# Expert gates built from bfloat16 one-hots of 8 tokens, one PSUM copy moved to ScalarE, and two activation steps moved forward

## The chip, the core and the metric

The kernel runs on one core of a Trainium2 chip. The metric is device time in microseconds (us) of one execution, the median of several. The engines are TensorE (PE, with its weight loads listed apart as PEld), VectorE (DVE), ScalarE (ACT), GpSimd (POOL) and SyncE (SP), which only issues DMAs here.

## The reference, cut to what matters

Two transformer blocks on 512 tokens of width 1024. The first has attention over 512 tokens and 16 meta tokens, then a feed-forward layer. The second has two more attentions and ends in PEER, a layer of 16384 experts, of which every token picks 16 in each of 8 heads:

```python
def _peer(h, w_pq, sub_keys, peer_u, peer_v):
    qp = (h @ w_pq).astype(jnp.float32).reshape(b, s, PEER_HEADS, 2, PEER_HALF)
    sc = jnp.einsum("bshpd,hpnd->bshpn", qp, sub_keys.astype(jnp.float32))
    s1, i1 = lax.top_k(sc[..., 0, :], PEER_TOPK)
    s2, i2 = lax.top_k(sc[..., 1, :], PEER_TOPK)
    cand = (s1[..., :, None] + s2[..., None, :]).reshape(b, s, PEER_HEADS, PEER_TOPK * PEER_TOPK)
    top_s, top_c = lax.top_k(cand, PEER_TOPK)
    e1 = jnp.take_along_axis(i1, top_c // PEER_TOPK, axis=-1)
    e2 = jnp.take_along_axis(i2, top_c % PEER_TOPK, axis=-1)
    expert = e1 * N_KEYS + e2                      # N_KEYS = 128
    gate = jax.nn.softmax(top_s, axis=-1)
    ...
    a = jnp.einsum("bcd,bchkd->bchk", h_c, peer_u[expert])
    w = gate * jax.nn.gelu(a)
    return jnp.einsum("bchk,bchkd->bcd", w, peer_v[expert])
```

The kernel computes PEER in two ways. For the first 128 tokens it fetches the picked rows one at a time ("sparse"). For the other 384 it computes all 16384 experts as dense matrix products and multiplies the activations by a dense matrix of gates, which is zero where an expert was not picked.

## The kernel before, in words

Everything is written in one order by hand, per engine; each engine runs its own instructions in that order. The places that the change touches are four.

**Attention of the first block** (65 to 330 us of the span). `turn1` transposes a block of probabilities on PE: four tiles of 128 keys into the bank `ps` (line 848), and the 16 meta keys into a free corner `m` of the PSUM bank that held the scores (line 846). ACT copies the four tiles to `pt` (line 850) and DVE copies the corner to `pm` (line 849). Until `pm` is copied the scores of a later step, which need that bank (lines 821 and 832), cannot be written.

**Dense gates** (1251 to 1482 us). `dense_gates` runs three times, `t` = 1, 2, 3, for 128 tokens each; below these are the first, second and third run. At the start PE transposes the expert numbers and the gates of the 128 tokens (lines 1840 and 1841) and ACT copies them to `et` (line 1843). Then come 32 steps of four tokens. For each token the gates are an outer product: a matrix with a 1 at (e1, k) for pick k, times a matrix with the gate at (e2, k). `ones` makes both. DVE makes the first for four tokens in one instruction (line 1854) and the second for three of the four tokens (line 1859, compare and multiply in one); ACT makes the second of the fourth token from two instructions (lines 1862 and 1863). All are float32. PE multiplies them (line 1876, one matmul call per token, four calls into one bank, each with a step of four in the output), and ACT copies the bank to `stage` (line 1878), which goes to DRAM as `gd`. `ones` runs two steps (`LA`) ahead of the products.

Between the steps `_merge` puts PE work of another kind, the first activations: per step `QW` = 1.0 us of it by a planner's figure, which gives two or three groups of three matmuls `ua` (lines 368 to 370). These bring with them the casts of streamed weights, `wh` on ACT (line 225) and `wl` on DVE (line 227), and their `ga` on ACT (line 1777). The expert numbers of the next run (`experts`, lines 1946 to 1952) are spread over the first two runs, and the sparse rows (line 1971) begin in the third.

**The main loop** (1482 to 2340 us). 64 rounds; each adds one group of experts to the output with 36 matmuls `yres` (line 2052) in six steps of `v_phase`. The gated activations of the next round are split into two parts for this: ACT makes `wh_` (line 2030) at step n = 2 and DVE makes `wl_` (line 2031) at n = 4, counted from 0, each from the entry `at[n]`. In between `tick` puts in sparse rows.

**Set-up.** `peer` makes a row of the numbers 0 to 127 with POOL's `iota` (line 1633).

Of the kernel before, what the change touches and what calls it, by code (L numbers as in the profile page):

```python
# [278 lines left out]
class Program:  # L279
# [561 lines left out]
    def turn1(self, p, pt, pm, s2):  # L841

        nc = self.nc
        ps = self.bank((P, 4, P), name="tp")
        m = s2[0:NMETA, 0, HK:HK + P]
        nc.tensor.transpose(out=m, in_=p[:, NTOK:NKEY], identity=self.ident)
        for j in range(4):
            nc.tensor.transpose(out=ps[:, j, :], in_=p[:, j * P:j * P + P], identity=self.ident)
        nc.vector.tensor_copy(out=pm[0:NMETA], in_=m)
        nc.scalar.copy(out=pt, in_=ps)  # L850
# [768 lines left out]
    def peer(self):  # L1619
# [11 lines left out]
        self.first_products(self.norm2, pss, pc["pq"], self.rest)  # L1631
        self.iota = self.ph.tile([P, P], F32, name="iota")
        nc.gpsimd.iota(self.iota, pattern=[[1, P]], base=0, channel_multiplier=0, allow_small_or_imprecise_dtypes=True)
        self.iota16 = self.ph.tile([P, 16, 8], BF16, name="iota16")
# [40 lines left out]
        for i in range(64):  # L1675
# [6 lines left out]
            if i < 63:  # L1682
# [8 lines left out]
                nxt = None  # L1691
            at = dict(zip((2, 4), todo[1:]))
            if i == 63:
# [90 lines left out]
    def gates(self, val, idx, found, keys):  # L1784
# [11 lines left out]
        for t in range(4):  # L1796
            yield from self.best_sums(val, top, topc, t)
            if t == 0:
                yield from self.softmax(top[:, 0:1], gt[:, 0:1], 2.5)
                self.where(topc[:, 0:1], sel[:, 0:1])  # L1800
                yield 2.0
                ee = self.tmp([P, 2, 128], name="ee")
                yield from self.experts(sel[:, 0], ixf[:, 0], ee)
                self.sgate = self.ph.tile([P, P], F32, name="sgate")
# [8 lines left out]
        yield GY[0]  # L1813
        ee = self.tmp([P, 2, 128], name="ee")
        soft = self.softmax(top[:, 1:4], gt[:, 1:4], 3.0)
        yield next(soft)
        yield from self.experts(sel[:, 1], ixf[:, 1], ee)
        yield from soft
        yield 3.0
        for t in range(1, 4):  # L1820
            now, more = ee, None
            if t < 3:
                ee = self.tmp([P, 2, 128], name="ee")
                more = self.experts(sel[:, t + 1], ixf[:, t + 1], ee)
            for i, us in enumerate(self.dense_gates(t, now, gt[:, t], 0)):
                if t == 3:
                    self.tick(QR)
                yield us
                if more and i % 6 == 3:
                    us = next(more, None)  # L1830
                    if us:
                        yield us
        self.ahead(0)

    def dense_gates(self, t, ee, gt, first):
# [5 lines left out]
        nc.tensor.transpose(out=ps[:, 2, :], in_=gt, identity=self.ident)  # L1841
        et = self.tmp([P, 4, P], name="et")
        nc.scalar.copy(out=et[:, 0:3], in_=ps)
        nc.scalar.mul(out=et[:, 3], in_=ps[:, 2], mul=-1.0)
        todo = [(blk, q) for blk in range(first, 4) for q in range(8)]
        hot = {}

        def ones(n):

            blk, q = todo[n]  # L1850
            tk = blk * 32 + q * 4
            o1 = self.tmp([P, 4, P], name="o1")
            o2 = self.tmp([P, 4, P], name="o2")
            nc.vector.tensor_tensor(out=o1, in0=self.iota.unsqueeze(1).to_broadcast([P, 4, P]),
                                    in1=et[:, 0, tk:tk + 4].unsqueeze(2).to_broadcast([P, 4, P]), op=OP.is_equal)
            for i in range(4):
                e2, g, ng = (et[:, j, tk + i:tk + i + 1] for j in (1, 2, 3))
                if i < 3:
                    nc.vector.tensor_scalar(out=o2[:, i, :], in0=self.iota, scalar1=e2, scalar2=g,
                                            op0=OP.is_equal, op1=OP.mult)  # L1860
                else:
                    nc.scalar.activation(out=o2[:, i, :], in_=self.iota, func=AF.Abs, bias=e2, scale=-1.0)
                    nc.scalar.activation(out=o2[:, i, :], in_=o2[:, i, :], func=AF.Relu, bias=g, scale=ng)
            hot[n] = o1, o2

        for n in range(LA):
            ones(n)
        for n, (blk, q) in enumerate(todo):
            if q == 0:
                stage = [self.slot([P, 64, 32], name="stage") for _ in range(2)]  # L1870
            if n + LA < len(todo):
                ones(n + LA)
            o1, o2 = hot.pop(n)
            pg = self.bank((P, P, 4), name="pg")
            for i in range(4):
                nc.tensor.matmul(out=pg[:, :, i], lhsT=o1[:, i, :], rhs=o2[:, i, :], start=True, stop=True)  # L1876
            for e in range(2):
                nc.scalar.copy(out=stage[e][:, :, q * 4:q * 4 + 4], in_=pg[:, e * 64:e * 64 + 64, :])
            if q == 7:
                for e in range(2):  # L1880
                    nc.scalar.dma_start(out=self.gd[t * 4 + blk - NS // 32, e], in_=stage[e])
            yield QW
# [54 lines left out]

    def experts(self, sel, ixf, ee):

        nc = self.nc  # L1940
        for a in range(2):
            eq = self.slot([P, 16, 16, 8], BF16, name="eq")
# [155 lines left out]
```

## Time and profile before

| | |
|---|---|
| median of 3 runs | 2361.22 us (2353.3 to 2362.54) |
| the profiled execution | 2359.9 us, of which the span of its instructions is 2358.2 us |
| mean granted clock of TensorE | 0.983 of full speed |
| PE busy | 2251.2 us (95%) |
| PEld busy | 1984.5 us (84%) |
| DVE busy | 1682.3 us (71%) |
| ACT busy | 983.1 us (42%) |
| POOL busy | 833.6 us (35%) |

PE and PEld overlap, and busy shares are averages over stages that differ. What the stages of the change look like is read from their own stretches of the trace, in us from the start of the span.

### The profile page before, as it was taken

How to read it: one execution, taken by the hardware profiler on the slowest of the kernel's cores; microseconds unless marked ns; L12 is line 12 of the kernel's file. 1: busy time of each engine (PE TensorE's matmuls, PEld its weight loads, DVE VectorE, ACT ScalarE, POOL GpSimd, SP SyncE). 2: the span in 40 equal slices, each digit the busy share in tenths (PEclk: the TensorE clock that was granted, in tenths of full speed). 3: DMA queues.
4: the chain of work that ended last, by engine and by line, in shares of the span. 5: the costliest groups of instructions: out<-in, count | busy, mean ns of one | idle time of the engine just before them, and what ended most of it. 6: DMA issues, size and time to landing. Idle time of an engine off the chain costs nothing.

```text
span 2358.2 us, 33496 instructions
## 1 busy us (share of the span) xinstructions
PE 2251.2 (95%) x12511; PEld 1984.5 (84%) x12511; DVE 1682.3 (71%) x3461; ACT 983.1 (42%) x1896; POOL 833.6 (35%) x666
## 2 busy tenths in 40 slices
PE   6999989999999998999998999999999999999998
PEld 5787868888889777788997999988888888888997
DVE  7565665766635547567998889577877778887776
ACT  4454453322224456543436777433333333333332
POOL 3231411020021235222340002356665666665553
PEclk9999999999999999999998999999999999999999
DMA  4111113645523101222354557998889989999885
GB/s 174 37 55 36 72 36 99 243 180 208 190 94 121 56 21 55 90 90 90 124 187 158 215 226 261 323 334 305 314 326 332 332 318 320 319 328 330 315 295 190
DMA packets 137698, 459.82 MB, mean 195 GB/s; under 512 B 10256, under 2 KB 62800, under 8 KB 105536
## 3 DMA queue, kind: packets, MB, share of 16 engines
q1 hardware_dynamic: 91120, 276.86, 33.2%
q0 software_dynamic: 37920, 138.31, 16.4%
q10 hardware_dynamic: 8496, 42.52, 4.5%
q8 instruction: 98, 1.61, 0.3%
q14 instruction: 64, 0.52, 0.1%
HBM read 415.13 MB, written 42.47 MB: 194 GB/s over the span
## 4 chain that ended last, share of the span: by engine, by line
PE 31%; DVE 11%; issue 6%; POOL 3%; ACT 2%; DMA 1%; ACTq 0%; POOLq 0%; DVEq 0%
PE yres L2052 15%; PE ua L370 4%; PE ua L368 4%; PE ua L369 4%; PE pg L1876 3%; POOL rows L1964 2%; DVE wl L227 1%; DVE ys L1986 1%; DVE rest L1749 1%; POOL ga L2029 1%; ACT wh L225 1%; DVE idx L1753 1%; DVE idx L1747 1%; DVE rows L1971 1%; DVE val L1751 1%
## 5 line engine op out<-in xcount | busy, mean ns | idle before, releaser
L227 DVE TENSOR_TENSOR wl<-raw,wh 128x1024 fp32r<-128x1024 f32 x345 | 480.6, 1411 | 313.3 <-ACT wh L225 312.7
L225 ACT CAST wh<-raw 128x1024 fp32r<-128x1024 f32 (+1 forms) x398 | 405.0, 1039 | 326.7 <-PE yres L2052 155.4
L368 PE MATMUL ua<-ah,wh 128*128 128x384 f32 x1024 | 353.2, 345 | 0.0
L370 PE MATMUL ua<-ah,wl 128*128 128x384 f32 x1024 | 345.0, 337 | 2.6 <-POOL wl L227 1.9
L369 PE MATMUL ua<-al,wh 128*128 128x384 f32 x1024 | 344.6, 337 | 0.0
L1964 POOL DMA_INDIRECT rows<-in_eu_dram,sidx x128 | 184.6, 1442 | 417.7 <-DVE rows L1971 380.8
L1964 POOL DMA_INDIRECT rows<-in_ev_dram,sidx x128 | 193.1, 1509 | 167.5 <-DVE ys L1986 141.1
L370 PEld LDWEIGHTS ua<-ah,wl 128*128 128x128 f32 x1024 | 193.6, 189 | 3.3 <-POOL wl L227 2.2
L369 PEld LDWEIGHTS ua<-al,wh 128*128 128x128 f32 x1024 | 194.2, 190 | 1.4
L368 PEld LDWEIGHTS ua<-ah,wh 128*128 128x128 f32 x1024 | 194.1, 190 | 1.4
L1986 DVE SCALAR_TENSOR_TENSOR ys<-rows,sact,ys 128x1024 f32<-128x1024 f32 x127 | 177.0, 1394 | 1.8
L227 POOL TENSOR_TENSOR wl<-raw,wh 128x1024 fp32r<-128x1024 f32 (+2 forms) x53 | 118.6, 2246 | 151.8 <-ACT wh L225 145.0
L1777 ACT ACTIVATE ga<-ua 128x384 f32<-128x384 f32 x128 | 63.3, 494 | 256.2 <-PE ua L370 252.4
L2029 POOL TENSOR_TENSOR ga<-ga,gt 128x384 f32<-128x384 f32 x128 | 157.8, 1256 | 21.4 <-DMA ga<-sd 20.2
L1971 DVE SCALAR_TENSOR_TENSOR rows<-rows,hn 128x1024 f32<-128x1024 f32 x128 | 159.8, 1272 | 0.0
L368 PE MATMUL pj<-wh,ah 128*128 128x512 f32 (+3 forms) x344 | 128.3, 373 | 9.7 <-ACT ah L521 9.3
L368 PE MATMUL gu<-ah,wh 128*128 128x512 f32 x352 | 137.4, 390 | 0.0
L370 PE MATMUL gu<-ah,wl 128*128 128x512 f32 x352 | 137.0, 389 | 0.0
L369 PE MATMUL gu<-al,wh 128*128 128x512 f32 x352 | 136.9, 389 | 0.0
L1194 POOL TENSOR_TENSOR xr<-xr,dr 128x512 f32<-128x512 f32 x12 | 20.0, 1670 | 294.9 <-DVE dr L1192 294.9
L370 PE MATMUL pj<-wh,al 128*128 128x512 f32 (+3 forms) x344 | 121.3, 353 | 0.1
L369 PE MATMUL pj<-wl,ah 128*128 128x512 f32 (+3 forms) x344 | 120.8, 351 | 0.0
(907 smaller groups left out, 5468.3 us busy)
## 6 DMA issues: line engine op xcount, KB each, us to landing
raw<-in_pu_dram SPq DMA_DIRECT2D x64, 1024.0 KB
raw<-in_pv_dram SPq DMA_DIRECT2D x64, 1024.0 KB
raw<-in_w_ada_dram SPq DMA_DIRECT2D x24, 1024.0 KB
gd<-stage ACTq DMA_DIRECT2D x24, 1024.0 KB
gt<-gd SPq DMA_DIRECT2D x32, 768.0 KB
raw<-in_w_gu_dram SPq DMA_DIRECT2D x22, 1024.0 KB
sd<-ga ACTq DMA_DIRECT2D x28, 384.0 KB
ga<-sd SPq DMA_DIRECT2D x28, 384.0 KB
```

The source lines that it names most:

```text
L225: nc.scalar.copy(out=hi[:, :w], in_=src)
L227: eng.tensor_tensor(out=lo[:, :w], in0=src, in1=hi[:, :w].bitcast(F32), op=OP.subtract)
L368: mm(out=out, lhsT=a[0], rhs=b[0], start=start, stop=False)
L369: mm(out=out, lhsT=a[0], rhs=b[1], start=False, stop=False)
L370: mm(out=out, lhsT=a[1], rhs=b[0], start=False, stop=stop)
L1777: nc.scalar.activation(out=ga[:, e * TD:e * TD + TD], in_=ps[:, 0:TD], func=AF.Gelu_apprx_tanh)
L1876: nc.tensor.matmul(out=pg[:, :, i], lhsT=o1[:, i, :], rhs=o2[:, i, :], start=True, stop=True)
L1964: nc.gpsimd.indirect_dma_start(out=row[i % NROW][0:NS], out_offset=None, in_=self.d["eu" if i < P else "ev"], in_offset=bass.IndirectOffse ...
L1971: nc.vector.scalar_tensor_tensor(out=row[i % NROW][0:NS], in0=row[i % NROW][0:NS], scalar=1.0, in1=self.hn[0:NS], op0=OP.mult, op1=OP.mult ...
L1986: nc.vector.scalar_tensor_tensor(out=ys, in0=row[i % NROW][0:NS], scalar=w, in1=ys, op0=OP.mult, op1=OP.add)
L2029: nc.gpsimd.tensor_tensor(out=a, in0=a, in1=gt[:, :, 2 * (g % 2) + e, :], op=OP.mult)
L2052: nc.tensor.matmul(out=o, lhsT=w[x][:, c], rhs=vv[e][y][:, s], start=i == 0 and e == x == y == 0, stop=i == 63 and e == y == 1)
```

## The change

- `turn1`: the copy of the meta corner goes from DVE to ACT, in front of ACT's copy of `pt`.
- Dense gates: the one-hots are bfloat16 and made for eight tokens at once, in tiles of [128 partitions, 128 numbers, 8 tokens]. The token is the innermost dimension, so one token's matrix, as PE reads it, has a step of eight elements of 2 bytes. The gate is split into three bfloat16 parts that add up to the float32 value, and each token has three matmuls that add up in PSUM, with one matrix loaded as weights each time. DVE makes all of them (lines 1855, 1856 and 1858 of the new kernel); ACT makes none. The split of the gates is made by DVE at the start of a run, from the bank with the transposed gates.
- The look-ahead is now one block of eight tokens, in four buffers out of the same nine.
- The expert numbers `ee` have a buffer of their own instead of one of the nine.
- `iota` becomes 128 numbers times 8, cast to bfloat16 by DVE.
- In the main loop the two parts are made at n = 1 and n = 3.

```diff
-        nc.vector.tensor_copy(out=pm[0:NMETA], in_=m)
+        nc.scalar.copy(out=pm[0:NMETA], in_=m)
...
-        self.iota = self.ph.tile([P, P], F32, name="iota")
-        nc.gpsimd.iota(self.iota, pattern=[[1, P]], base=0, channel_multiplier=0, allow_small_or_imprecise_dtypes=True)
+        self.iota8 = self.ph.tile([P, P, 8], BF16, name="iota8")
+        it = self.slot([P, P, 8], name="it8")
+        nc.gpsimd.iota(it, pattern=[[1, P], [0, 8]], base=0, channel_multiplier=0, allow_small_or_imprecise_dtypes=True)
+        nc.vector.tensor_copy(out=self.iota8, in_=it)
...
-            at = dict(zip((2, 4), todo[1:]))
+            at = dict(zip((1, 3), todo[1:]))
...
-        et = self.tmp([P, 4, P], name="et")
+        et = self.tmp([P, 5, P], BF16, name="et")
         nc.scalar.copy(out=et[:, 0:3], in_=ps)
-        nc.scalar.mul(out=et[:, 3], in_=ps[:, 2], mul=-1.0)
+        for j in (2, 3):
+            nc.vector.tensor_tensor(out=ps[:, 2, :], in0=ps[:, 2, :], in1=et[:, j], op=OP.subtract)
+            nc.vector.tensor_copy(out=et[:, j + 1], in_=ps[:, 2, :])
...
-            tk = blk * 32 + q * 4
-            o1 = self.tmp([P, 4, P], name="o1")
-            o2 = self.tmp([P, 4, P], name="o2")
-            nc.vector.tensor_tensor(out=o1, in0=self.iota.unsqueeze(1).to_broadcast([P, 4, P]),
-                                    in1=et[:, 0, tk:tk + 4].unsqueeze(2).to_broadcast([P, 4, P]), op=OP.is_equal)
-            for i in range(4):
-                e2, g, ng = (et[:, j, tk + i:tk + i + 1] for j in (1, 2, 3))
-                if i < 3:
-                    nc.vector.tensor_scalar(out=o2[:, i, :], in0=self.iota, scalar1=e2, scalar2=g,
-                                            op0=OP.is_equal, op1=OP.mult)
-                else:
-                    nc.scalar.activation(out=o2[:, i, :], in_=self.iota, func=AF.Abs, bias=e2, scale=-1.0)
-                    nc.scalar.activation(out=o2[:, i, :], in_=o2[:, i, :], func=AF.Relu, bias=g, scale=ng)
-            hot[n] = o1, o2
+            tk = slice(blk * 32 + q * 4, blk * 32 + q * 4 + 8)
+            o = [self.tmp([P, P, 8], BF16, name="o") for _ in range(4)]
+            of = lambda j: et[:, j, tk].unsqueeze(1).to_broadcast([P, P, 8])
+            nc.vector.tensor_tensor(out=o[0], in0=self.iota8, in1=of(0), op=OP.is_equal)
+            nc.vector.tensor_tensor(out=o[3], in0=self.iota8, in1=of(1), op=OP.is_equal)
+            for j in (1, 2, 3):
+                nc.vector.tensor_tensor(out=o[j], in0=o[3], in1=of(j + 1), op=OP.mult)
+            hot[n] = o
...
-            if n + LA < len(todo):
-                ones(n + LA)
-            o1, o2 = hot.pop(n)
+            if n % 2 == 0:
+                if n + 2 < len(todo):
+                    ones(n + 2)
+                o = hot.pop(n)
             pg = self.bank((P, P, 4), name="pg")
             for i in range(4):
-                nc.tensor.matmul(out=pg[:, :, i], lhsT=o1[:, i, :], rhs=o2[:, i, :], start=True, stop=True)
+                k = n % 2 * 4 + i
+                for j in (1, 2, 3):
+                    nc.tensor.matmul(out=pg[:, :, i], lhsT=o[0][:, :, k], rhs=o[j][:, :, k], start=j == 1, stop=j == 3)
...
-    def experts(self, sel, ixf, ee):
+    def experts(self, sel, ixf):
+        self.ee = ee = self.ph.tile([P, 2, 128], F32, tag="ee", name="ee")
```

How this moves the instructions shows in the order on three engines. On PE, this is the start of the first run and its first step before (the numbers after `o` are buffers):

```order
L1840 MATMUL et<-ident,ee 128x128 x2
L1841 MATMUL et<-ident,tg 128x128
L1876 MATMUL pg<-o_12423,o_12422 128x128 x4
L368 MATMUL ua<-ah,wh 128x384
L369 MATMUL ua<-al,wh 128x384
```

and this is the same place now, up to the second of the step's twelve pairs of a weight load and a matmul:

```order
L1838 MATMUL et<-ident,ee 128x128 x2
L1839 MATMUL et<-ident,tg 128x128
L1873 LDWEIGHTS o
L1873 MATMUL pg<-o 128x128
L1873 LDWEIGHTS o
L1873 MATMUL pg<-o 128x128
```

Four float32 calls, which the trace shows as eight passes, became twelve bfloat16 pairs; as before nothing else stands between the transposes and the first product, and the `ua` groups after it are the same. On DVE, this is the start of the first run before:

```order
L1936 TENSOR_TENSOR tg<-tg,s 128x384
L227 TENSOR_TENSOR wl<-raw,wh 128x1024
L1854 TENSOR_TENSOR o_12422<-iota,et 128x512
L1859 TENSOR_SCALAR o_12423<-iota,et 128x128 x3
L1854 TENSOR_TENSOR o_12430<-iota,et 128x512
```

and now:

```order
L1933 TENSOR_TENSOR tg<-tg,s 128x384
L227 TENSOR_TENSOR wl<-raw,wh 128x1024
L1844 TENSOR_TENSOR et<-et 128x128
L1845 CAST et<-et 128x128
L1844 TENSOR_TENSOR et<-et 128x128
L1845 CAST et<-et 128x128
L1855 TENSOR_TENSOR o<-iota_10472,et 128x1024
L1856 TENSOR_TENSOR o<-iota_10472,et 128x1024
L1858 TENSOR_TENSOR o<-o,et 128x1024 x3
```

Four instructions for four tokens became five larger ones for eight, with the split in front. On DVE in the main loop, where `wl_` is the second part of the activations, `wl` the lower part of a streamed weight and `ys` a sparse row, this is a stretch of one of the last rounds before:

```order
L227 TENSOR_TENSOR wl<-raw_20861,wh 128x1024 x2
L1986 SCALAR_TENSOR_TENSOR ys<-rows,sact,ys 128x1024
L227 TENSOR_TENSOR wl<-raw,wh 128x1024
L1986 SCALAR_TENSOR_TENSOR ys<-rows,sact,ys 128x1024 x3
L2031 TENSOR_TENSOR wl__21058<-ga,wh__21057 128x768
L1986 SCALAR_TENSOR_TENSOR ys<-rows,sact,ys 128x1024
```

and the same stretch now:

```order
L227 TENSOR_TENSOR wl<-raw_21304,wh 128x1024 x2
L1984 SCALAR_TENSOR_TENSOR ys<-rows,sact,ys 128x1024
L227 TENSOR_TENSOR wl<-raw,wh 128x1024
L1984 SCALAR_TENSOR_TENSOR ys<-rows,sact,ys 128x1024 x2
L2029 TENSOR_TENSOR wl__21501<-ga,wh__21500 128x768
L1984 SCALAR_TENSOR_TENSOR ys<-rows,sact,ys 128x1024 x2
```

The part stands one sparse row further forward. ACT's order in the main loop is the same as before, since nothing of ACT's stood between n = 1 and n = 2.

## Rows read from the trace of the kernel before

**Rows 1.** Windows, the three runs: length, busy us of each engine, clock, DMA share, GB/s

```profile
1251.50:1331.50 80.00, 76.23 (x503) 75.61 (x504) 65.02 (x151) 58.91 (x150) 0.00 (x0) 0.93 0.48 179
1331.50:1407.60 76.10, 72.49 (x508) 71.90 (x507) 64.01 (x150) 58.70 (x150) 0.00 (x0) 1.00 0.54 210
1407.60:1482.50 74.90, 67.95 (x459) 65.29 (x458) 69.15 (x163) 57.43 (x148) 15.15 (x12) 0.98 0.75 269
```

**Rows 2.** Timeline of PE, first run: start us, duration us, line, output, inputs, count

```profile
1302.08 0.34 PE L370 MATMUL ua<-ah,wl 128*128 128x384 f32 x1
1302.25 1.05 PE L1876 MATMUL pg<-o,o 128*128 128x128 f32 x8
1303.06 0.42 PE L368 MATMUL ua<-ah,wh 128*128 128x384 f32 x1
1303.32 0.34 PE L369 MATMUL ua<-al,wh 128*128 128x384 f32 x1
1303.49 0.34 PE L370 MATMUL ua<-ah,wl 128*128 128x384 f32 x1
...
1304.19 1.05 PE L1876 MATMUL pg<-o,o 128*128 128x128 f32 x8
```

**Rows 3.** Timeline of DVE, first run: start us, duration us

```profile
1300.45 0.68 DVE L1854 TENSOR_TENSOR o<-iota,et 128x512 f32<-128x512 f32 x1
1301.05 0.86 DVE L1859 TENSOR_SCALAR o<-iota,et 128x128 f32<-128x128 f32 x3
1301.82 0.69 DVE L1854 TENSOR_TENSOR o<-iota,et 128x512 f32<-128x512 f32 x1
```

**Rows 4.** Waits in the three runs: who for whom, us in total, times, longest

```profile
DVE wl L227 <- ACT wh L225: 28.1, 18, 4.8
PE pg L1876 <- DVE o L1859: 14.2, 11, 3.9
```

**Rows 5.** Start of the second run, timeline of all engines

```profile
1331.75 0.27 PE L1841 MATMUL et<-ident,tg 128*128 128x128 f32 x1
1332.94 0.48 ACT L1843 COPY et<-et 128x384 f32<-128x384 f32 x1 [1.60 <-PE et L1841]
1333.45 0.69 DVE L1854 TENSOR_TENSOR o<-iota,et 128x512 f32<-128x512 f32 x1 [4.00 <-ACT et L1843]
1334.54 1.13 PE L1876 MATMUL pg<-o,o 128*128 128x128 f32 x8 [2.52 <-DVE o L1859]
```

**Rows 6.** bfloat16 weights and matmuls, by tile (ns min/median/max) and timeline

```profile
L1567 PEld LDWEIGHTS <-identb x32: 95/97/99, 800.1 to 901.5; 128*128 128x128 bf16 x32
L1567 PE MATMUL s<-maskb,identb x32: 219/224/230, 800.1 to 901.6; 128*128 128x128 bf16 x32
800.11 0.28 PE L1567 MATMUL s<-maskb,identb 128*128 128x128 bf16 x2
```

**Rows 7.** Groups by form, DVE from 1160 to 1410 us: count, busy us, mean ns, idle before

```profile
L1947 DVE TENSOR_TENSOR eq<-eq,si 128x2048 bf16<-128x2048 bf16 x8 | 9.8, 1226 | 0.3
L1951 DVE TENSOR_TENSOR eq<-eq 128x1024 bf16<-128x1024 bf16 x8 | 5.5, 687 | 0.1
L1921 DVE TENSOR_TENSOR si<-im,ov 128x384 bf16<-128x384 f32 x1 | 1.9, 1906 | 0.0
L1920 DVE TENSOR_TENSOR im<-im,cf 128x384 f32<-128x384 f32 x1 | 0.6, 560 | 0.0
```

**Rows 8.** Groups of ACT from 1250 to 1482 us

```profile
L1863 ACT ACTIVATE o<-o,et 128x128 f32<-128x128 f32 x96 | 47.4, 494 | 3.2
L1862 ACT ACTIVATE o<-iota,et 128x128 f32<-128x128 f32 x96 | 39.4, 410 | 3.3 <-ACT stage L1878 1.8 <-DVE o L1859 1.2 <-ACT wh L225 0.3
```

**Rows 9.** First block's attention, 60 to 340 us: PE's waits, and ACT's small copy

```profile
PE s L832 <- DVE pm L849: 7.6, 7, 3.5
PE s L821 <- DVE pm L849: 4.8, 5, 2.0
L707 ACT CAST mix<-ot 128x128 fp32r<-128x128 f32 x16 | 4.2, 260 | 0.0
```

**Rows 10.** Main loop: a window, and one round's waits in PE's timeline

```profile
1700.00:1800.00 100.00, 98.79 (x479) 86.72 (x478) 78.75 (x90) 33.05 (x40) 62.41 (x46) 1.00 0.89 324
1547.91 0.49 PE L2052 MATMUL yres<-wh,wh__15359 128*128 128x512 f32 x1 [0.71 <-ACT wh__15359 L2030]
1548.90 0.50 PE L2052 MATMUL yres<-wh,wl__15360 128*128 128x512 f32 x1 [0.50 <-DVE wl__15360 L2031]
```

**Rows 11.** POOL's iota, by line

```profile
L1633 POOL IOTA iota<- x1: 232/232/232, 1048.1 to 1048.1; 128x128 f32 x1
```

More of the change, by code (lines that the diff above doesn't have):

```diff
@@ L1801, in gates @@
                 yield 2.0
-                ee = self.tmp([P, 2, 128], name="ee")
-                yield from self.experts(sel[:, 0], ixf[:, 0], ee)
+                yield from self.experts(sel[:, 0], ixf[:, 0])
+                ee = self.ee
                 self.sgate = self.ph.tile([P, P], F32, name="sgate")
@@ L1813, in gates @@
         yield GY[0]
-        ee = self.tmp([P, 2, 128], name="ee")
         soft = self.softmax(top[:, 1:4], gt[:, 1:4], 3.0)
         yield next(soft)
-        yield from self.experts(sel[:, 1], ixf[:, 1], ee)
+        yield from self.experts(sel[:, 1], ixf[:, 1])
         yield from soft
@@ L1820, in gates @@
         for t in range(1, 4):
[L1821 to L1825, printed above, removed]
+            more = self.experts(sel[:, t + 1], ixf[:, t + 1]) if t < 3 else None
+            for i, us in enumerate(self.dense_gates(t, self.ee, gt[:, t], 0)):
                 if t == 3:
@@ L1850, in ones @@
             blk, q = todo[n]
-            tk = blk * 32 + q * 4
-            o1 = self.tmp([P, 4, P], name="o1")
-            o2 = self.tmp([P, 4, P], name="o2")
-            nc.vector.tensor_tensor(out=o1, in0=self.iota.unsqueeze(1).to_broadcast([P, 4, P]),
-                                    in1=et[:, 0, tk:tk + 4].unsqueeze(2).to_broadcast([P, 4, P]), op=OP.is_equal)
-            for i in range(4):
-                e2, g, ng = (et[:, j, tk + i:tk + i + 1] for j in (1, 2, 3))
-                if i < 3:
-                    nc.vector.tensor_scalar(out=o2[:, i, :], in0=self.iota, scalar1=e2, scalar2=g,
-                                            op0=OP.is_equal, op1=OP.mult)
-                else:
-                    nc.scalar.activation(out=o2[:, i, :], in_=self.iota, func=AF.Abs, bias=e2, scale=-1.0)
-                    nc.scalar.activation(out=o2[:, i, :], in_=o2[:, i, :], func=AF.Relu, bias=g, scale=ng)
-            hot[n] = o1, o2
-        for n in range(LA):
-            ones(n)
+            tk = slice(blk * 32 + q * 4, blk * 32 + q * 4 + 8)
[6 more added lines that the diff above has]
+            hot[n] = o
+        ones(0)
         for n, (blk, q) in enumerate(todo):
```

## The prediction

> **What bounds the kernel now.** I read the stretches of the three dense-gate runs first, since most of the change lies there, then the timelines of PE and DVE inside them, then the waits. In the windows of the runs [rows 1] PE is busy 76.2 of 80.0, 72.5 of 76.1 and 68.0 of 74.9 us, so 14.3 us of the 231.0 us are without a matmul. DVE is busy 65.0, 64.0 and 69.2 us and ACT 58.9, 58.7 and 57.4 us. The reader is to see that PE sets the pace of the first two runs, and that DVE is close behind it in the third, where the sparse rows begin. PE's timeline [rows 2] gives one step: the products start at 1302.25, the next step's at 1304.19, 1.94 us apart. Of this the eight float32 passes of `pg` take 0.81 us, up to the first `ua`, and that one holds the next up by 0.26 instead of 0.17 us; I count 0.81 + 0.085 = 0.895 us per step, or 0.11 us a pass. The rest is `ua`, which the change leaves alone. DVE's timeline [rows 3] gives what a step costs there: from one compare to the next 1.37 us. Of the 14.3 us of idle PE, 14.2 were waits for DVE's one-hots [rows 4], the longest of them at the starts of the runs: in the second run PE ends its transposes and starts its products 2.8 us later [rows 5].
>
> **PE's products.** Each step loses 8 float32 passes and gets 12 bfloat16 pairs of load and matmul; there are 3 x 32 = 96 steps. The price of a pair is the number on which the forecast hangs. No matmul of the trace reads an operand with a step, so I bound it. From below: two bfloat16 pairs with packed operands that follow each other take 0.28 us together, one alone 0.224 [rows 6], so the second started 0.056 us after the first. Then a step takes 12 x 0.056 + 0.085 = 0.757 us, 0.14 less than now, and the runs are 13 us shorter. From above: load and matmul each at half that rate, and one after the other, 4 x 0.056 = 0.22 us a pair. Then a step takes 2.73 us, and the runs are 176 us longer. Between them I take half the packed rate with load and matmul side by side, 0.11 us. The reason is what a step of 16 bytes does on another engine: DVE writes 128x384 bfloat16 with this very step in 1906 ns, while the same size in packed float32 takes 560 ns [rows 7]. That is a write, and on DVE, so it only tells me that the step is unlikely to be free. The float32 pass, which reads 4 bytes side by side where the new one reads 2 out of 16, sits at the same 0.11 us. With it a step takes 12 x 0.11 + 0.085 = 1.405 us, 0.51 more than now: 96 x 0.51 = **+49 us**.
>
> [...]
>
> **DVE's one-hots.** Eight tokens took 2 x 1.37 = 2.74 us. They now take five instructions on 128x1024 bfloat16. One such took 687 ns, and the same kind with an operand repeated over a dimension 1226 ns for twice the size [rows 7], so repeating costs nothing and 687 ns is the price. Independent instructions start about 0.085 us before the end of the one ahead (0.68 us long, but 0.60 apart, in [rows 3]); the third of the five needs the second and starts after it. That makes 4 x 0.60 + 0.72 = 3.12 us, 0.19 us more per step, 18 us over the 96 steps. In the first two runs DVE's 65 us become some 72 of 80 and stay hidden behind PE, the more so with slower products. DVE also waits 28 us for ACT's `wh` in these runs [rows 4], time that it can use. In the third run, 69.2 + 32 x 0.19 + 1.2 = 76.5 us of DVE is over PE's 68.0 if PE does not get slower; that goes into the rival below.
>
> **Starts of the runs.** PE stands still from the transposes to the first products. Now the gates are split first: two subtractions and two casts, each needing the last, 4 x 0.3 = 1.2 us (a small DVE instruction with its wait: the 344 ns of line 1859, three in 0.86 us [rows 3]). Then come 3.12 us for eight tokens before the last of the first matmuls, where 1.1 us lay between the copy's end at 1333.42 and the products at 1334.54 [rows 5]. That is 4.3 instead of 1.1, +3.2 us at each of three starts: **+10 us**. Nothing covers it, as nothing stands between transposes and products. What goes away again: of the 14.3 us idle about 8 were such starts, some 2.5 us each as in [rows 5]; the other 6 were DVE late inside a run, and with slower products DVE is early. I take **-5 us**.
>
> **ACT in the runs.** 47.4 + 39.4 = 86.8 us of one-hots leave it [rows 8]. ACT is not what ends PE's waits, so this is worth nothing by itself; what it frees are the `wh` casts, for which DVE waits, not PE.
>
> **The meta copy.** In the attention PE waits 7.6 + 4.8 = 12.4 us for DVE's `pm` [rows 9]. ACT gets the copy right behind the transposes and in front of `pt`, for which it has to wait for PE anyway; a 128x128 copy of ACT takes 260 ns [rows 9], and if the four other transposes are done by then, it delays `pt`, the values behind it, and PE. Between -12 us (all waits gone) and +12 us (48 copies of 260 ns, all on the path) I take **-6 us**: the wait goes, but about half of it comes back at the next scores, which need DVE's maxima.
>
> **The main loop.** PE is busy 98.79 of 100 us [rows 10], so some 9 us over the 860 us of the loop are all that could be won. In the round shown the waits are 0.71 us for ACT's part, whose place on ACT does not change, and 0.50 us for DVE's, which directly follows ACT's. Where DVE's part stood behind a sparse row it comes one row, 1.2 us, earlier; the row behind it comes later, and POOL's next fetch with it, which could cost as much. Between -5 and +3 us I take **-2 us**. The larger `iota` is eight times 0.23 us [rows 11] at most, ahead of the keys' load that a later product needs; I put it at nothing, as its own result is first used in the runs, 200 us later, and at 2 us if the keys are waited for.
>
> **Sum.** 49 + 10 - 5 - 6 - 2 = +46 us. The profiled execution took 2359.9 us, 1.7 us over its span and 1.3 us under the median shown, so I predict 2406 us.
>
> **Rivals.** *The step is free on PE* (0.056 us a pair): PE has 13 us less to do in the runs and waits 10 us more at the starts. Runs one and two end some 5 us earlier in all, as DVE's lateness shrinks with ACT out of the one-hots. Run three is bound by DVE at 76.5 us and its wait for the transposed gates, 80 instead of 74.9 us: +5. Left are the -6 and -2: about 2352 us, no change by the measure below. It becomes faster, not merely the same, if DVE does not bind the third run and the attention gets most of its 12.4 us: 2359.9 - 5 - 10 - 4 = 2341. For it: [rows 6] show bfloat16 loads at 95 ns, so cheap loads exist; against it: those operands are packed. The point from which it decides is a pair of about 0.075 us: below it DVE's work, not PE's, is the longer in the third run.
>
> *The step costs half of that again* (0.083 us, midway from 0.056 to 0.11): a step of 1.08 us, 0.186 more than now, +18, and with 10 - 4 - 8 it ends at 2376 us. [...]
>
> *Load and matmul stand in each other's way* (0.22 us): +176 + 10 - 5 - 8 = +173, 2533 us. [...] Against it: in the float32 passes a load of 0.1 us and a matmul hide each other [rows 2].
>
> **How the numbers follow.** A measurement of this kernel tells changes of over 0.5% (12 us) from none. Half rate, my forecast: 0.42, all slower. Free step: 0.38, of it 0.21 the same and 0.17 faster. Midway: 0.10, of it 0.06 slower and 0.04 the same. Both in each other's way: 0.10, slower. Together 0.17 faster, 0.25 the same, 0.58 slower. The range leaves out the last case and the best quarter of the free step, and takes in pairs of up to 0.13 us: 2346 to 2434 us. The likeliest case alone, at 0.10 to 0.125 us, spans 2392 to 2425.
>
> **What would show it.** The products of a step (line 1873) take 1.3 to 1.5 us, against 0.81; the three runs together 280 to 290 us against 231, the middle of each run with PE hardly idle. One-hots (lines 1855 to 1858) at 0.6 to 0.7 us each. At each start PE idle for 5 to 6 us. Waits for `pm` gone from PE's list in the attention, with other waits in their place. The main loop within 5 us. The prediction is wrong if a pair takes 0.06 us, if the weight loads and not the matmuls set the pace, or if the attention gains more than 12 us because the scores start early all along its chain.

## The result, and the profile after

The changed kernel takes 2529.96 us (median; 2529.44 to 2530.73) where the kernel before took 2361.88 us beside it: a ratio of 1.071 [1.070, 1.073], +168 us. The prediction was 2406 us, with a range of 2346 to 2434. The profiled execution has a span of 2529.0 us against 2358.2, +170.8 us.

Where they lie, the windows of the three gate runs show first (columns as in [rows 1]):

```profile
1243.10:1384.00 140.90, 136.54 (x633) 100.47 (x634) 74.35 (x107) 35.09 (x85) 0.00 (x0) 0.96 0.28 104
1384.00:1524.20 140.20, 135.88 (x636) 99.80 (x634) 73.22 (x106) 34.81 (x85) 0.00 (x0) 0.98 0.29 112
1524.20:1657.60 133.40, 127.15 (x584) 90.98 (x583) 78.42 (x119) 33.36 (x83) 13.04 (x12) 0.96 0.45 157
```

The runs take 414.5 us against 231.0, +183.5. They start at 1243.1 instead of 1251.5 (-8.4), and what follows them takes 2529.0 - 1657.6 = 871.4 instead of 875.7 us (-4.3): together +170.8. The reader is to see that PE is busy in all but 14.9 us of them, nearly as little idle as before (14.3). So it is not waiting; its work is longer. PE's timeline of one step says which work:

```profile
1301.05 3.01 PE L1873 MATMUL pg<-o 128*128 128x128 bf16 x12
1303.70 0.54 PE L368 MATMUL ua<-ah,wh 128*128 128x384 f32 x1
1304.07 0.34 PE L369 MATMUL ua<-al,wh 128*128 128x384 f32 x1
```

Twelve pairs take 2.65 us from their start to the first `ua`, 0.221 us a pair; the first `ua` holds the next up by 0.37 instead of 0.17 us. That is 2.85 us a step against 0.895 [rows 2], and 96 x 1.95 = +187 us, within 4 us of what the windows show. Counted over all matmuls of the runs, from start to start and without the waits, the products take 254.3 instead of 81.9 us and the `ua` 167.4 instead of 156.6: +172 and +11.

The other engines did what was foretold. The groups of DVE in the runs (count, busy us, mean ns, idle before and what ended it):

```profile
L1858 DVE TENSOR_TENSOR o<-o,et 128x1024 bf16<-128x1024 bf16 x144 | 95.3, 690 | 5.8 <-DVE o L1856 0.5
L1855 DVE TENSOR_TENSOR o<-iota,et 128x1024 bf16<-128x1024 bf16 x48 | 33.0, 688 | 30.0 <-PE pg L1873 30.0
```

A one-hot takes 690 ns, and DVE now waits 30 us for PE to give buffers back. The start of the first run, all engines:

```profile
1243.62 0.48 ACT L1842 CAST et<-et 128x384 bf16<-128x384 f32 x1 [3.79 <-PE et L1839]
1244.13 0.30 DVE L1844 TENSOR_TENSOR et<-et 128x128 f32<-128x128 f32 x1
1245.33 0.68 DVE L1855 TENSOR_TENSOR o<-iota,et 128x1024 bf16<-128x1024 bf16 x1
1246.65 2.02 DVE L1858 TENSOR_TENSOR o<-o,et 128x1024 bf16<-128x1024 bf16 x3
1247.39 0.39 PE L1873 MATMUL pg<-o 128*128 128x128 bf16 x1 [3.81 <-DVE o L1858]
1248.72 0.63 PE L1873 MATMUL pg<-o 128*128 128x128 bf16 x2 [0.34 <-DVE o L1858]
```

From the copy's end at 1244.10 to the last of the first token's three matmuls at 1248.72 lie 4.6 us; the prediction had 4.3. In the attention, PE's waits are now:

```profile
PE s L846 <- DVE s L940: 6.9, 4, 3.3
PE s L846 <- ACT prob L884: 6.0, 5, 2.2
PE s L832 <- ACT pm L849: 1.1, 2, 0.7
```

The 12.4 us for `pm` [rows 9] became 1.1, and 6.0 us of waits for ACT's `prob` are new. These stand in front of the transposes (line 846), which need the exponentials that ACT makes at line 884; ACT now has the copies to do as well.

### The profile page after: what moved, and what is told of

Same layout as the page of the kernel before. It is cut to its first block, busy times and chain, and to the rows that moved or that the text cites. A ratio compares the mean times of both kernels' runs of the same rounds, so it can differ in the third digit from the quotient of the medians.

```text
span 2529.0 us, 33916 instructions
## 1 busy us (share of the span) xinstructions
PE 2428.1 (96%) x12895; PEld 2062.5 (82%) x12895; DVE 1691.2 (67%) x3282; ACT 920.9 (36%) x1749; POOL 845.4 (33%) x666
## 4 chain that ended last, share of the span: by engine, by line
PE 38%; DVE 9%; issue 6%; POOL 4%; ACT 1%; DMA 0%; POOLq 0%; DVEq 0%; ACTq 0%
PE yres L2050 14%; PE pg L1873 11%; PE ua L368 4%; PE ua L370 4%; PE ua L369 4%; POOL rows L1962 3%; DVE wl L227 1%; POOL ga L2027 1%; DVE rest L1751 1%; DVE idx L1755 1%; DVE idx L1749 1%; DVE val L1753 0%; DVE val L1747 0%; DVE ys L1984 0%; DVE rows L1969 0%
## 5 line engine op out<-in xcount | busy, mean ns | idle before, releaser
L368 PE MATMUL ua<-ah,wh 128*128 128x384 f32 x1024 | 364.6, 356 | 0.0
L1873 PE MATMUL pg<-o 128*128 128x128 bf16 x1152 | 288.9, 416 | 14.9 <-DVE o L1858 14.9
L1873 PEld LDWEIGHTS <-o 128*128 128x128 bf16 x1152 | 160.2, 147 | 112.9 <-issue 16.2
L2027 POOL TENSOR_TENSOR ga<-ga,gt 128x384 f32<-128x384 f32 x128 | 169.4, 1345 | 27.3 <-DMA ga<-sd 26.1
L1875 ACT COPY stage<-pg 128x256 f32<-128x256 f32 x192 | 62.3, 376 | 301.0 <-PE pg L1873 300.5
L1984 DVE SCALAR_TENSOR_TENSOR ys<-rows,sact,ys 128x1024 f32<-128x1024 f32 x127 | 168.4, 1326 | 1.6
```

Of the source, the lines that this page charges most:

```text
L368: mm(out=out, lhsT=a[0], rhs=b[0], start=start, stop=False)
L1873: nc.tensor.matmul(out=pg[:, :, i], lhsT=o[0][:, :, k], rhs=o[j][:, :, k], start=j == 1, stop=j == 3)
L1984: nc.vector.scalar_tensor_tensor(out=ys, in0=row[i % NROW][0:NS], scalar=w, in1=ys, op0=OP.mult, op1=OP.add)
L2027: nc.gpsimd.tensor_tensor(out=a, in0=a, in1=gt[:, :, 2 * (g % 2) + e, :], op=OP.mult)
```

## The experiments

The open question was the pair: 0.221 us where 0.11 had been taken. Two theories to begin with. One, the rival's: load and matmul take turns, each at some 0.11 us. The other: the matmul alone is slow, because of the step of its moving operand, the one-hot with the gates, and the load lies beside it. Most kernels below are the changed kernel with other tiles for the one-hots, so that PE reads the loaded operand at a step of `sw` and the moving one at `sm` (8 and 8 in the change). DVE has the same number of instructions of the same size; where `sw` and `sm` differ, one of its two compares reads two of eight repeated numbers and takes 1.07 to 1.10 instead of 0.69 us. The main lines, with `sw` and `sm` for the numbers:

```diff
-            o = [self.tmp([P, P, 8], BF16, name="o") for _ in range(4)]
+            o = [self.tmp([P, 8 // w, P, w], BF16, name="o") for w in (sw, sm, sm, sm)]
...
-                    nc.tensor.matmul(out=pg[:, :, i], lhsT=o[0][:, :, k], rhs=o[j][:, :, k], start=j == 1, stop=j == 3)
+                    nc.tensor.matmul(out=pg[:, :, i], lhsT=o[0][:, k // sw, :, k % sw],
+                                     rhs=o[j][:, k // sm, :, k % sm], start=j == 1, stop=j == 3)
```

Each timeline below is of one step; the median of all 96 steps of the kernel lies within 0.02 us of it.

**Which operand.** Three kernels: `sw, sm` = 4, 4, then 2, 8, then 8, 2.

> The changed kernel with its one-hot tiles laid out as [128 partitions, 2 blocks, 128 numbers, 4 tokens], so that PE reads both operands with a step of 4 elements (8 bytes) and not 8 (16 bytes); DVE has the same number of instructions of the same size. Theory A (a 16-byte step of the operands is what slows the pair from 0.056 to 0.221 us): two neighbours of the read share 16 bytes again, the pair goes to 0.056 to 0.08 us, a step's 12 pairs to 0.7 to 1.0 us, and the kernel to 2340 to 2370 us. Rival B (the step of the PSUM output, written three times, is what slows it): the pair stays at 0.22 us and the kernel at 2530 us. Rival C (the price grows with the step, halving with it): 0.11 us a pair, 2400 us.

> The changed kernel with only the loaded weights (the first one-hot) at a step of 2 elements and the moving operand still at 8. If load and matmul are slow one after the other (the rival of the prediction, each at half rate), the pair falls to about 0.17 us (0.056 + 0.11), 2475 us. If the moving operand alone sets it (four times the packed time, the load hidden), it stays at 0.22 us, 2530 us. If the weights alone set it, 0.06 to 0.08 us, 2345 to 2370 us. Rival B (PSUM step): 0.22 us.

> The mirror: weights at a step of 8, the moving operand at 2. Load and matmul one after the other, each at half rate: 0.17 us, 2475 us. The moving operand alone: 0.06 to 0.08 us, 2345 to 2370 us. The weights alone: 0.22 us, 2530 us. Rival B (PSUM step): 0.22 us.

Measured: 2404.96 us (ratio 1.018 [1.017, 1.020]), 2524.58 us (one run) and 2410.72 us (one run). PE's timelines, in this order:

```profile
1302.97 1.59 PE L1880 MATMUL pg<-o 128*128 128x128 bf16 x12
1304.32 0.43 PE L368 MATMUL ua<-ah,wh 128*128 128x384 f32 x1
```

```profile
1301.80 2.91 PE L1880 MATMUL pg<-o 128*128 128x128 bf16 x12
1304.36 0.54 PE L368 MATMUL ua<-ah,wh 128*128 128x384 f32 x1
```

```profile
1302.46 1.53 PE L1880 MATMUL pg<-o 128*128 128x128 bf16 x12
1303.75 0.42 PE L368 MATMUL ua<-ah,wh 128*128 128x384 f32 x1
```

The reader divides the distance of the two starts by 12: 0.112, 0.213 and 0.108 us a pair. It is the moving operand. With a near-packed load the pair still takes 0.213 of 0.221 us, so the two are not taking turns. But with the moving operand at step 2 it takes 0.108 us, not the 0.06 to 0.08 expected if that operand alone counted.

**A second price.** Two kernels with `sw, sm` = 2, 2 and 1, 1 (the second with packed operands).

> Both operands at a step of 2 elements (4 bytes), everything else as in the changed kernel. The step of 4 for both gave 0.112 us a pair, a step of 8 for the weights alone with the moving operand at 2 gave 0.108, a step of 8 for the moving operand alone 0.213. Theory A (the moving operand costs four times the packed time at a step of 8 and twice at 4; the weights at a step of 8 cost twice): 0.056 to 0.08 us a pair now, 12 pairs in 0.7 to 1.0 us, 2340 to 2365 us, with DVE then the longer engine in the runs. Rival D (0.108 us is a floor of such pairs whatever the step, from three matmuls into one place or from load and matmul in turn): 0.108 us, 2400 to 2410 us.

> Both operands packed ([8 tokens, 128 numbers] with a token's numbers side by side). DVE then reads the token's value repeated along the innermost dimension and may lose its double rate (1.1 us and not 0.69 an instruction), which would make DVE the longer engine, so the total says little; the pair is what counts. Theory A: 0.056 us, or what step 2 has. Rival D: 0.108 us.

Step 2: 2399.17 us, ratio 1.016 [1.014, 1.018]; twelve pairs 1.24 us, 0.103 each. Packed: 2493.69 us (one run), also 0.103 a pair. The timelines, in this order:

```profile
1301.16 1.49 PE L1880 MATMUL pg<-o 128*128 128x128 bf16 x12
1302.40 0.42 PE L368 MATMUL ua<-ah,wh 128*128 128x384 f32 x1
```

```profile
1304.72 1.49 PE L1880 MATMUL pg<-o 128*128 128x128 bf16 x12
1305.96 0.42 PE L368 MATMUL ua<-ah,wh 128*128 128x384 f32 x1
```

So 0.103 us is not the operand's step; something else sets it, as two packed pairs had been 0.056 apart [rows 6]. The time of the packed kernel is mostly DVE's, as its groups show: a token's numbers lie side by side there, the gate is repeated along the innermost dimension, and an instruction takes 1223 instead of 690 ns; 690 ns for 1024 bfloat16 columns had been twice the rate of float32, 0.68 us for 512 [rows 3]. PE waits 81.6 us for one-hots, against 20.3 at step 2.

```profile
L1865 DVE TENSOR_TENSOR o<-o,et 128x1024 bf16<-128x1024 bf16 x144 | 172.1, 1223 | 5.8 <-DVE o L1863 0.5
```

**Is it the load of 128 columns, and does the price go by 16-byte pieces?** Each matmul cut in two of 64 columns (every other one), each with its own load, in the tiles of step 2; and the same with the moving operand at a step of 16 elements, which spreads 64 columns over the same bytes as the change's 128.

```diff
-                for j in (1, 2, 3):
-                    nc.tensor.matmul(out=pg[:, :, i], lhsT=o[0][:, k // 2, :, k % 2],
-                                     rhs=o[j][:, k // 2, :, k % 2], start=j == 1, stop=j == 3)
+                for c in (0, 1):
+                    for j in (1, 2, 3):
+                        nc.tensor.matmul(out=pg[:, c::2, i], lhsT=o[0][:, k // 2, :, k % 2],
+                                         rhs=o[j][:, k // 2, c::2, k % 2], start=j == 1, stop=j == 3)
```

> The step-2 kernel (12 pairs in 1.24 us, 0.103 us each, 2399 us) with every matmul cut into two of 64 columns (even and odd ones), each with its own load of the same 128x128 weights: 24 pairs a step. Theory E (the floor of 0.103 us is the load of 128 weight columns, the matmul hidden behind it): 0.103 us a pair still, 2.47 us a step, 2517 us. Rival F (load and matmul in turn, 0.05 + 0.053): 0.077 us, 1.85 us, 2458 us. Rival G (the moving columns or the sums in PSUM set it): 0.05 us, 1.24 us, 2399 us.

> Weights at a step of 2, the moving operand's 128 columns at a step of 8 read in two matmuls of 64 columns at a step of 16 elements (32 bytes); with 128 columns at a step of 8 a pair took 0.213 us and the kernel 2525 us. Theory H (the read costs by the span that it covers, 0.213 us for the 2 KB of 128 columns x 16 bytes): 64 columns still cover 2 KB, 0.213 us a pair, 24 of them 5.1 us, 2770 us. Rival I (it costs by the lines of 16 bytes that it touches, one per column at both steps): 0.107 us a pair, 2.56 us, 2525 us.

2413.83 and 2535.55 us (one run each). The timelines, in this order:

```profile
1302.32 1.63 PE L1881 MATMUL pg<-o 128*128 128x64 bf16 x24
1303.76 0.42 PE L368 MATMUL ua<-ah,wh 128*128 128x384 f32 x1
```

```profile
1303.70 3.00 PE L1881 MATMUL pg<-o 128*128 128x64 bf16 x24
1306.45 0.43 PE L368 MATMUL ua<-ah,wh 128*128 128x384 f32 x1
```

24 pairs with 24 loads of 128 columns take 1.44 us, 0.060 each, so no load needs 0.103. With a column in every second 16 bytes a pair of 64 columns takes 0.115 us, 1.8 ns a column. At step 8 it was 0.213 / 128 = 1.7 ns. So what counts here is the number of 16-byte pieces that the columns touch, 1.7 to 1.8 ns each, not the bytes between first and last; the expectation that went by bytes (twice this) fell.

**The bank.** The changed kernel with the bank written packed and operands still at step 8; then step 2 with the packed bank and without the sums (every matmul starts anew, so two of the three parts of each gate are left out); then step 2 with the packed bank and the sums.

```diff
-            pg = self.bank((P, P, 4), name="pg")
+            pg = self.bank((P, 4, P), name="pg")
...
-                    nc.tensor.matmul(out=pg[:, :, i], ...
+                    nc.tensor.matmul(out=pg[:, i, :], ...
...
-                nc.scalar.copy(out=stage[e][:, :, q * 4:q * 4 + 4], in_=pg[:, e * 64:e * 64 + 64, :])
+                nc.scalar.copy(out=stage[e][:, :, q * 4:q * 4 + 4], in_=pg[:, :, e * 64:e * 64 + 64].rearrange("p i c -> p c i"))
```

> The changed kernel with the products written side by side into the PSUM bank ([4 tokens, 128] and not a step of 4 floats), and ACT's copy to stage reading it with a step. The operands keep their step of 8. Theory A: the pair stays at 0.22 us; only ACT's copy may change, which waits 300 us for PE anyway: 2525 to 2535 us. Rival B: the pair falls to 0.11 us or below, 2345 to 2410 us.

> The step-2 kernel with the products packed in PSUM and none of them added up: each of a token's three matmuls starts anew and overwrites the last, so the gates lack two of their three parts. Theory E: 0.103 us a pair as before, 2390 to 2410 us. Rival G: without the sums and without the output's step the pair falls to 0.056 us, 2340 to 2360 us.

> All four operands at step 2, the sums of the three parts as in the change, and the bank written packed (4 x 128 instead of 128 x 4). Theory P (the second price, 0.103 us a pair at step 2, is set by the step of 4 floats at which a product is written into its bank): the pair falls to 0.057 us, 12 pairs take 0.68 us, VectorE's five instructions bind a step, about 2381 us. Theory S (it is set by adding three products in place in the bank): the pair stays at 0.103 us, 12 pairs 1.24 us, about 2400 us.

At step 8 the packed bank changes nothing for the pair (0.222 us), and the kernel takes 2562.72 us (one run), where 2525 to 2535 had been expected; the last section comes back to it. At step 2 it nearly halves the pair, without the sums (2381.26 us, one run, for an expected 2340 to 2360) and with them (2376.88 us, one run; the kernel before took 2359.47 beside it). The last one's timeline:

```profile
1305.84 0.87 PE L1880 MATMUL pg<-o 128*128 128x128 bf16 x12
1306.52 0.42 PE L368 MATMUL ua<-ah,wh 128*128 128x384 f32 x1
```

0.68 us for twelve, 0.057 each. The second price is the step of four floats in the bank, 0.103 against 0.057 us; the sums cost nothing, as without them twelve pairs also take 0.68 us. And with a pair at this price the change is still a loss: the kernel's runs take 262 us (1243.8 to 1506.0), against 231.0. Most of the 31 us are waits of PE for one-hots, 40.8 us against 14.2 before [rows 4]. The waits in these runs, of PE, DVE and ACT:

```profile
PE pg L1880 <- DVE o L1865: 40.8, 55, 5.7
DVE wl L227 <- ACT wh L225: 25.2, 15, 5.0
ACT stage L1883 <- PE pg L1880: 137.5, 76, 6.2
```

**How many columns in 16 bytes, and what a load pays.** With the packed bank, `sw, sm` = 4, 4 and 8, 2.

> All four operands at step 4 (two columns in a line of 16 bytes), the bank written packed. Theory L (the moving operand pays about 1.7 ns for each line that a column touches, and with two columns in a line that is 0.85 ns a column): the pair stays at 0.107 to 0.112 us, 12 pairs 1.29 to 1.35 us, about 2400 us. Theory M (two columns in a line already give the full rate, and the 0.112 us at step 4 was the second price, that of the bank's step or of the sums): the pair falls to the 0.057 us of packed operands, 12 pairs 0.68 us, about 2381 us, provided the bank's step is what sets that second price.

> The loaded operand at step 8, the moving one at step 2, the bank written packed. Theory L (a load pays little for its lines, as the 0.108 us beside 0.103 with the bank's step says): the pair takes 0.057 to 0.065 us, 12 pairs 0.68 to 0.78 us, about 2381 us. Theory W (a load pays for its lines too, and lay hidden under the second price of 0.103 us): the pair takes 0.10 us or more, about 2400 us.

2399.19 and 2398.4 us (one run each). The timelines, in this order:

```profile
1301.38 1.59 PE L1880 MATMUL pg<-o 128*128 128x128 bf16 x12
1302.72 0.43 PE L368 MATMUL ua<-ah,wh 128*128 128x384 f32 x1
```

```profile
1304.19 0.98 PE L1880 MATMUL pg<-o 128*128 128x128 bf16 x12
1304.98 0.42 PE L368 MATMUL ua<-ah,wh 128*128 128x384 f32 x1
```

Two columns in 16 bytes cost 0.112 us a pair, twice the 0.057 of four columns. The load's step of 8 costs 0.066 against 0.057. The second kernel's total missed its expectation (2381) by 17 us, and is 21.5 us above the kernel with both at step 2. Of these, 1152 pairs x 0.009 = 10 us are the pair's. The slower compare (1087 instead of 685 ns) gives DVE 48 x 0.4 = 19 us more, but PE's waits for one-hots grew only from 40.8 to 44.9 us. Its first run also starts 4.4 us later, by no more than such starts differ from kernel to kernel (the next part has their range).

| moving operand's step, columns | 16-byte pieces touched | pair, us, bank at a step of 4 floats | pair, us, bank packed | ns a piece |
|---|---|---|---|---|
| 1, 128 | 16 | 0.103 | | |
| 2, 128 | 32 | 0.103 | 0.057 | 1.77 |
| 4, 128 | 64 | 0.112 | 0.112 | 1.74 |
| 8, 128 (load at 2) | 128 | 0.213 | | 1.66 |
| 16, 64 | 64 | 0.115 (step of 8 floats) | | 1.79 |

The last three rows carry the count by 16-byte pieces, at 1.66 to 1.79 ns each. Pieces of 8 bytes would make a column at step 4 as dear as one at step 8, and pieces of 32 bytes would make one at step 16 twice as dear as one at step 8; neither is so. At step 2 the pair takes what packed pairs take (0.056 us [rows 6]), so there the columns themselves may set it.

**The small parts alone.** The kernel before with ACT's copy alone, with the steps 1 and 3 alone, and with both:

```diff
-        nc.vector.tensor_copy(out=pm[0:NMETA], in_=m)
+        nc.scalar.copy(out=pm[0:NMETA], in_=m)
...
-            at = dict(zip((2, 4), todo[1:]))
+            at = dict(zip((1, 3), todo[1:]))
```

> The kernel before with only the meta copy on ACT. If the 8.4 us that the first gate run starts earlier are the copy's: 2352 to 2354 us, ratio 0.9965. If ACT's copy delays pt and the gain has another source: no change or slower, 2358 us or more.

> The kernel before with only the activations' parts at n = 1 and 3. The two edits together gave 0.9954 and the copy alone 0.9972; if they add up, 0.998 to 0.9985, 2357 us, the main loop 3 to 4 us shorter. If the edit is worth nothing by itself: 0.9995 to 1.0005.

> The kernel before with only the two small edits: the meta copy on ACT and the activations' parts at n = 1 and 3. In the changed kernel's trace the first gate run starts 8.4 us earlier and the main loop is 4.2 us shorter. If both come from these edits: 12.6 us less, 2347 to 2350 us, a ratio of 0.9945 to 0.995. If they are a by-product of the slow gate runs (weights loaded further ahead, for example): less than 6 us.

2355.38 us, ratio 0.9972 [0.9962, 0.9983]; 2357.73 us, 0.9986 [0.9975, 0.9997]; 2350.38 us, 0.9954 [0.9941, 0.9968]. The copy gains 4 to 9 us and the steps 1 to 6. PE's waits in the attention with the copy alone:

```profile
PE s L846 <- ACT prob L884: 5.5, 5, 1.8
PE s L832 <- ACT pm L849: 1.1, 2, 0.6
```

About half of the 12.4 us comes back as waits for ACT, as in the changed kernel. A single pair of traces says little of a part this small: the first gate run starts between 1239.9 and 1248.2 us in the sixteen kept traces with the copy, and between 1249.0 and 1253.5 in the three without. The steps show more evenly: from the first `yres` to the end lie 847.8 to 849.1 us in the sixteen traces with them, 851.2 to 852.5 in the three without. Of this gain the waits show less than 1 us: with the steps alone PE still waits four times 0.7 us and four times 0.5 us for the parts, and only the two waits of 0.4 us are gone. The rest lies in the spacing of the `yres`: without the waits, 2304 of them take 532.4 us before and 529.0 with the steps alone. What holds them apart stays open.

**The bank in the kernel before.** Its float32 pass cost the price of a pair with the bank's step, 0.81 / 8 = 0.10 us against 0.103. Both kernels keep the float32 one-hots; the second has the copy and the steps too.

> The kernel before with one edit: its float32 one-hots as they are, the bank of the gates written packed (4 x 128 instead of 128 x 4). Its eight passes take 0.81 us a step, 0.10 us each, the price that bfloat16 pairs at step 2 had with the same bank (0.103 us) and lost with the packed one (0.057 us). Theory B (the bank's step sets the price of the float32 pass too): eight passes take 0.45 to 0.50 us, 0.057 to 0.06 each, PE has 96 x 0.33 = 32 us less to do, of which VectorE's 65 us of 80 and the starts let some 10 to 25 show: 2335 to 2350 us. Theory D (the float32 pass is held by its own load of weights): eight passes stay at 0.81 us and the time within 0.5% of before.

> The kernel before with the change's copy of the meta corner, its steps 1 and 3, and the bank written packed; the one-hots stay float32. By theory B 10 to 25 us under copy and steps alone (2350 us), so 2325 to 2340 us; by theory D the same 2350 us. If VectorE's one-hots come too late for the faster passes, the pass is shorter and the waits for one-hots grow from 14 us by as much.

2361.61 us, ratio 1.0003 [0.9993, 1.0013], and 2350.49 us, 0.9953 [0.9938, 0.9968]. Eight passes take 0.81 us, as in [rows 2], in the first of the two kernels:

```profile
1302.16 1.05 PE L1876 MATMUL pg<-o,o 128*128 128x128 f32 x8
1302.97 0.42 PE L368 MATMUL ua<-ah,wh 128*128 128x384 f32 x1
```

So the bank's step does not set the price of the float32 pass. That its own load does was the other theory and was not shown. The best kernel found is the one before with the copy and the steps, at 2350.4 us, with either bank.

## Why the prediction was wrong, point by point

**The price of a pair** is the step that failed: "Between them I take half the packed rate with load and matmul side by side, 0.11 us." Load and matmul do lie side by side (the twelve loads of the step at 1304.94 us last to 1307.46, its matmuls to 1307.95), but the matmul runs at about a quarter of the packed rate, 0.213 us of the pair's 0.221 against 0.057. The term of +49 us measures +187 by the step, of which 11 us are the first `ua`, held up by 0.20 and not 0.085 us. The prediction gave no reason for a half that a row bore out. Its own row for a step of 16 bytes, DVE's 1906 against 560 ns [rows 7], is a factor of 3.4, and 3.4 x 0.056 = 0.19 us would have come much nearer; it was set aside as a write on another engine, and no run shows that the two prices have one cause. The float32 pass at 0.11 us, read beside it as support, has another limit, which stays open: it does not move with the bank, and its operands are packed.

**The two prices behind it.** No row ahead of the prediction shows either for a matmul. The moving operand's goes by the 16-byte pieces touched: with the packed bank, two columns in a piece cost 0.112 us a pair and four 0.057. The other is that of the step of four floats in the bank, 0.103 against 0.057 us at step 2. It does not show where the operand is slower still: 0.112 us with either bank at step 4, 0.221 and 0.222 at step 8.

**The rivals.** "Load and matmul stand in each other's way" had the right price, 0.22 us, and 2533 us for a measured 2530, but by luck, as the mechanism is wrong: a pair with the load at step 2 still takes 0.213 us. The free step was put at 2352 us; with a pair at 0.057 us and everything else of the change the kernel takes 2376.9. There the prediction took DVE to bind only the third run. In fact PE waits for one-hots 55 times over the three runs, 40.8 us, although DVE is busy in only 223 of their 262 us. DVE itself waits 25.2 us there for ACT's `wh`, nearly the 28 us that the prediction called "time that it can use", and ACT waits 137.5 us for the products before its copies to `stage`. So no engine is full: each holds to its written order, and the wait goes round from PE to ACT to DVE and back. This is read from the waits; no run changed that order, or made the five one-hots in smaller pieces. The forecast's reasoning was therefore too kind to the change twice.

**The rest of the sum held.** One-hots take 690 ns each (687 taken), though the last three follow each other at 0.67 and not 0.60 us, so that eight tokens take 3.34 us for 3.12. The starts plus the idle time that goes away came to +0.6 us, from 14.3 to 14.9 us of idle PE, where +5 was taken: the three starts grew from 8.0 to 14.9 us, +7 for +10, and the other 6 us went whole, for -5. ACT's one-hots were worth nothing here, as said: ACT is busy 103 instead of 175 us in the runs, and PE sets the pace. The meta copy brought -8.4 us in the changed kernel and -4 to -9 alone, for -6. Half of the wait came back as foretold, but in front of the next transposes and for ACT's exponentials, not at the next scores for DVE's maxima. The main loop brought -4.3 us in the changed kernel and -1 to -6 alone, for -2. With 0.221 us in place of 0.11, the prediction's own step is 12 x 0.221 + 0.085 = 2.737 us and its sum +177 + 10 - 5 - 6 - 2 = +174, or 2534 us.

## What to carry to other kernels

When an operand of a matmul is laid out with a step, count the 16-byte pieces that its columns touch and price the moving operand by them (here 1.7 ns each), before counting matmuls; fold the layout so that at least four bfloat16 columns share a piece, which here cost VectorE nothing (690 ns at steps 2, 4 and 8). Then look at the step on the output's side too (here 0.103 against 0.057 us a pair). And before a saving on one engine is booked, run it in the mind to its end: here even a pair at the packed operands' 0.057 us left a slower kernel, 2376.9 against 2359.5 us, because the one-hots came too late (40.8 us of PE's waits).

## What the runs showed of the hardware that was not expected

The load of weights hardly minds a step: 128 columns at step 8 cost 0.008 to 0.009 us more a pair than at step 2, twice measured (0.221 against 0.213, 0.066 against 0.057), while the moving operand's same step costs 0.16.

With the packed bank at step 8 the pair stayed the same, and the one run was 33 us slower than the changed kernel. Windows of the same 40 us in the changed kernel and then with the packed bank (length, PE busy, clock, DMA share, GB/s):

```profile
1280.00:1320.00 40.00, 40.00 (x191) 1.00 0.33 132
```

```profile
1280.00:1320.00 40.00, 40.00 (x169) 0.80 0.25 99
```

PE has no idle time in either, but the granted clock is 0.80 instead of 1.00, a mean of stretches at two levels, 1.00 and 0.50. Over the runs it is 0.82 against 0.97, they take 445 against 414.5 us, and PE's waits for one-hots are the same 14.9 us. So the extra time goes with the clock. Why the clock is lower stays open, and one run does not show that the packed bank brought it about.

But this run shows where the clock counts. A stretch with a granted clock of 0.50 (window as above, then PE's timeline):

```profile
1301.00:1307.00 6.00, 6.00 (x23) 0.50 0.36 149
1302.31 3.02 PE L1873 MATMUL pg<-o 128*128 128x128 bf16 x12
1304.97 0.68 PE L368 MATMUL ua<-ah,wh 128*128 128x384 f32 x1
1305.45 0.53 PE L369 MATMUL ua<-al,wh 128*128 128x384 f32 x1
1305.77 0.53 PE L370 MATMUL ua<-ah,wl 128*128 128x384 f32 x1
```

Twelve pairs take 2.66 us, the 2.65 of the changed kernel at a clock of 1.00, while the `ua` stand 0.32 instead of 0.17 us apart. Of all 96 steps the 20 that lie wholly at the lower level take 2.65 us in the median, the 57 wholly at the higher 2.64. At step 8, then, the pair's time does not go with the granted clock, and that of the `ua` does. This fits the moving operand's step as what sets the pair. From the first product to the last the products take 256.0 us, in the changed kernel 255.8; the `ua` take 172.0 instead of 142.8.
